# Six and five row buffers in place of three for the gathered experts of a two-layer trunk

## The chip, the cores and the metric

The kernel runs on one core of a Trainium2 chip. The core has a matrix engine (TensorE, PE in the profile; its weight loads are PEld), a vector engine (VectorE, DVE), a scalar engine (ScalarE, ACT), GpSimd (POOL) and SyncE (SP), and 16 DMA engines that move data between HBM and the on-chip buffer SBUF. Each engine works off its own list of instructions in order; semaphores make one list wait for another or for a transfer. The metric is the time on the device in microseconds, lower is better.

## The reference

Two layers (DEPTH = 2) of width 1024 run over 512 latent tokens and 256 context tokens. Each layer has token mixers and then a feed-forward part that picks 16 experts per head from 16384, with 8 heads, so 128 experts per token:

```python
q = (xc @ w_q).reshape(PEER_CHUNK, PEER_HEADS, 2, PEER_HALF)
s = jnp.einsum('thid,hikd->thik', q, sub_keys)
...                                    # top 16 of each half, then top 16 of the sums
u = u_emb[eidx]
hid = jax.nn.gelu(jnp.einsum('td,thkd->thk', xc, u))
wgt = gate * hid
return jnp.einsum('thk,thkd->td', wgt, v_emb[eidx])
```

`u_emb` and `v_emb` are tables of 16384 rows of 1024 float32 numbers. The context tokens are needed by the first layer's feed-forward part and by the second layer's keys and values; only the 512 latent tokens are returned.

## The kernel before

The kernel computes in float32 by splitting each operand into a high part (rounded on ACT, L93) and a low part (the rest, on DVE, L94), and by three matmuls for each product (L98 to L100, `mm3`). So each chunk of weights costs one ACT and one DVE instruction before PE can use its low part: `wlo` for projections, `ul` for the first expert matrix and `vl` for the second.

The feed-forward part is computed in two ways at once.

- **Dense.** For most tokens (all 512 in the first layer, 384 in the second) PE multiplies by all 16384 experts: `hidden` streams `peer_u` in 128 chunks of 512 KB (`uraw`, split to `uh`, `ul`), and `values` streams `peer_v` (`vraw`, split to `vh`, `vl`). `weigh` multiplies the hidden activations by a gate matrix, zero for the experts that were not picked, and splits the result into `wh`, `wl`.
- **Gathered.** For the 256 context tokens of the first layer and the last 128 latent tokens of the second, `gathered` fetches only the picked rows. A tile is 128 tokens. For each head it fetches 16 times one row of `peer_u` per token, and then 16 times one row of `peer_v`; one fetch is 128 rows of 4 KB, so 524 288 bytes. POOL issues the fetch as an indirect DMA (L855). DVE multiplies a `peer_u` row with the token and sums it up (L868), ACT applies the gelu, and DVE adds the weighted `peer_v` row to an accumulator (L876 for the first, L878 for the others). That is 256 fetches a tile, 512 in the first layer and 256 in the second.

In the first layer the gathered tiles lie beside the mixers of the latent tokens, their keys and top-k, `hidden` and `values`. In the second layer the gathered tile lies beside keys, gates, `hidden` and `values` of the latent tokens. In the second layer `experts` computes the first 20 chunk groups of `hidden` to memory; then it runs `hidden` for two groups at a time in turn with `values` for the two before (the loop over `c` with pool `vb`), and last `values` for the 20 stored groups (pool `vc`).

The program is written as tiles and pools; a tile pool with `bufs=3` gives three places in turn, and a new tile in a place waits until the last reader of the old one is done. A scheduler then fixes the order of each engine's list, by a model of times and by priorities. The gathered tiles have the lowest priority (`self.prio(late)` with late = 40000): their instructions go where the model finds an engine free. On the chip these lists are fixed, so a DVE instruction of the gathered tiles that waits for its row holds up all that stands behind it on DVE.

Of the kernel before, what the change touches and what calls it, by code (L numbers as in the profile page):

```python
# [21 lines left out]
F32 = mybir.dt.float32  # L22
# [10 lines left out]
P = 128  # L33
D = 1024
KT = D // P
# [34 lines left out]
class Net:  # L70
# [778 lines left out]
    def gathered(self, l, tiles, gp, gq, nat, late):  # L849

        nc, a = self.nc, self.a

        def fetch(t, idx, s):
            r = gp.tile([P, D], F32, tag="row", name="row", bufs=3)
            nc.gpsimd.indirect_dma_start(out=r, out_offset=None, in_=a[t],  # L855
                                         in_offset=bass.IndirectOffsetOnAxis(ap=idx[:, s:s + 1], axis=0))
            return r

        for row, idx, g, hsrc, i, dst in tiles:
            with self.prio(late):  # L860
                x = gp.tile([P, D], F32, name="gx", bufs=1)
                nc.sync.dma_start(x, nat[row:row + P, :])
                acc = gp.tile([P, D], F32, name="gacc", bufs=1)
                for h in range(8):
                    hid = gp.tile([P, 16], F32, name="ghid", bufs=2)
                    for k in range(16):
                        r = fetch("peer_u", idx, h * 16 + k)
                        nc.vector.scalar_tensor_tensor(out=r, in0=r, scalar=1.0, in1=x, op0=OP.mult, op1=OP.mult,  # L868
                                                       accum_out=hid[:, k:k + 1])
                    w = gp.tile([P, 16], F32, name="gw", bufs=2)  # L870
                    nc.scalar.activation(w, hid, AF.Gelu_apprx_tanh)
                    nc.vector.tensor_tensor(w, w, g[:, h * 16:h * 16 + 16], op=OP.mult)
                    for k in range(16):
                        r = fetch("peer_v", idx, h * 16 + k)
                        if h == 0 and k == 0:
                            nc.vector.tensor_scalar(acc, r, w[:, k:k + 1], None, op0=OP.mult)  # L876
                        else:
                            nc.vector.scalar_tensor_tensor(acc, r, w[:, k:k + 1], acc, op0=OP.mult, op1=OP.add)  # L878
            res = gp.tile([P, KT, P], F32, tag="row", name="gres", bufs=3)
            nc.sync.dma_start(res, hsrc.rearrange("(k p) t -> p k t", p=P))  # L880
            tr = gq.tile([P, 4, P], F32, tag="gtr", name="gtr", bufs=1)
            for k in range(KT):
                nc.tensor.transpose(tr[:, k % 4], acc[:, k * P:(k + 1) * P], self.ident)
                nc.vector.scalar_tensor_tensor(res[:, k], tr[:, k % 4], self.modT[l][:, 40 + k, i:i + 1], res[:, k], op0=OP.mult, op1=OP.add)
            nc.sync.dma_start(dst.rearrange("(k p) t -> p k t", p=P), res)
# [10 lines left out]
    def run(self):  # L896
        nc, tc, a = self.nc, self.tc, self.a
        dt = lambda name, shape=(D, NT): tc.dram_tile(list(shape), F32, name=name)
        L = range(DEPTH)
        self.pd, self.od, self.md = [[dt(f"{n}{l}") for l in L] for n in ("pd", "od", "md")]  # L900
        self.qd, self.kd = [[dt(f"{n}{l}", (NH, P, 2, NT)) for l in L] for n in ("qd", "kd")]
        self.ld = [dt(f"ld{l}", (NH, P, NT)) for l in L]
        self.vd = [dt(f"vd{l}", (2, NH, P, NT)) for l in L]
        self.hmid = [dt(f"hmid{l}") for l in L]
        self.hout = dt("hout")
        self.natd = [dt("natd0", (NC, D)), dt("natd1", (P, D))]
        self.gd = dt("gd", (NX // 32, P, P * 32))
        self.hidd = dt("hidd", (32, P, 4 * NX))
        self.EC, self.stored = 2, 20
        X, Cx = Stream(0, NX, 0), Stream(NX, NC, 1)  # L910
        with ExitStack() as root:
            self.consts(self.pool(root, "consts"))
            ges = eh = h = None
            for l in L:
                ges, eh, h = self.trunk(l, X, Cx, ges, eh, h)
                ges, eh, h = self.ffn(l, ges, eh, h)
            eh.close()
            ges.close()
# [205 lines left out]
    def experts(self, l, y, up, uq, eu, e2):  # L1124


        n, EC, S = y.n, self.EC, self.stored
        with ExitStack() as es:
            self.hidden(l, y, up, uq, range(S), 12000)
            acc = self.pool(es, f"acc{l}").tile([P, KT, n], F32, name="acc")  # L1130
            va, vq = self.pool(es, f"va{l}"), self.pool(es, f"vq{l}", 1, PSUM)
            with ExitStack() as ev:
                vb = self.pool(ev, f"vb{l}")
                for c in range(S, 32 + EC, EC):
                    if c < 32:
                        ge = self.hidden(l, y, up, uq, range(c, c + EC), 0, True)
                    if c > S:
                        cs = range(c - EC, c)
                        self.values(l, n, cs, self.weigh(l, n, va, cs, had), lambda dq: (vb, 3, vb, EC + 2), vq, acc, c == S + EC)
                    had = ge  # L1140
                eu.close()
                e2.close()
            vb = self.pool(es, f"vc{l}", side="right")
            for c in range(0, S, EC):
                cs = range(c, c + EC)
                self.values(l, n, cs, self.weigh(l, n, va, cs), lambda dq: (vb, 3, vb, EC + 2), vq, acc, False,
                            vb if c == S - EC else None)
# [73 lines left out]
```

## Time and profile before

| | before |
|---|---|
| median of 3 runs | 5116.54 us (5113.34 to 5140.52) |
| profiled execution | 5126.48 us |
| its span in the trace | 5124.7 us |
| PE busy in the span | 4846.5 us |
| DVE busy in the span | 3946.3 us |
| data moved | 1280.77 MB, 250 GB/s in the mean |

The profiled execution is 9.9 us above the median, and its span leaves 1.8 us of it outside. In a row of the wait view, the engine and instruction on the left waited for what stands right of the arrow; then come the total in us, the number of waits and the longest. In a row of windows the busy time of each engine in that stretch is given, with the number of its instructions, then the granted clock of PE (1.00 is 2.4 GHz, the lower level of 1.2 GHz counts as 0.5), the busy share of the 16 DMA engines and the data rate. In a timeline row stand the start, the duration, the instruction, and in brackets the idle time before it and what ended it.

### The profile page before, as it was taken

The numbers are of one execution on the slowest core, as the hardware profiler recorded it, in microseconds if no ns is written. First come the engines' busy times: TensorE is split into PE (matmuls) and PEld (weight loads), VectorE is DVE, ScalarE is ACT, GpSimd is POOL, SyncE is SP. The second block draws the span as 40 slices with busy tenths as digits, with TensorE's granted clock in tenths as the row PEclk, the third lists the DMA queues.
The fourth block names the chain that finished last, engine by engine and source line by source line (L and its number), as shares of the span: only waits on it lengthen the run. The fifth ranks groups of instructions, "written<-read, shape, count | busy, mean of one in ns | idle before, by whom it ended". The sixth has DMA issues, their size and how long they took to land.

```text
span 5124.7 us, 74008 instructions
## 1 busy us (share of the span) xinstructions
PE 4846.5 (95%) x27373; PEld 4187.1 (82%) x27373; DVE 3946.3 (77%) x7996; ACT 1984.5 (39%) x2970; POOL 1199.9 (23%) x1060
## 2 busy tenths in 40 slices
PE   8999999798799999989999999999999999899999
PEld 5689787576588788768888879888679889899999
DVE  5468785977799998568888766777459999787885
ACT  4346665222233344323222334555334344332333
POOL 0012000144433343243334100100000433244320
PEclk9999999899899999999999999999899999999999
DMA  8668554488888888999999734543355888988995
GB/s 308 239 201 237 179 169 129 145 271 276 281 302 270 297 300 323 323 315 320 342 335 337 261 114 161 175 135 118 120 169 173 282 297 329 319 313 292 335 330 177
DMA packets 509419, 1280.77 MB, mean 250 GB/s; under 512 B 42880, under 2 KB 225024, under 8 KB 500736
## 3 DMA queue, kind: packets, MB, share of 16 engines
q1 hardware_dynamic: 302816, 669.35, 38.7%
q0 software_dynamic: 132352, 449.90, 26.1%
q10 hardware_dynamic: 73888, 156.79, 8.2%
q8 instruction: 215, 3.52, 0.3%
q14 instruction: 148, 1.21, 0.1%
HBM read 1098.13 MB, written 177.73 MB: 249 GB/s over the span
## 4 chain that ended last, share of the span: by engine, by line
PE 47%; DMA 14%; issue 11%; DVE 9%; POOL 3%; ACT 1%; POOLq 0%; DVEq 0%; ACTq 0%; SPq 0%
DMA row<-peer_v,ix 8%; PE dps L100 6%; PE dps L99 6%; PE dps L98 6%; DMA row<-peer_u,ix 5%; PE mm L98 4%; PE mm L100 4%; PE mm L99 4%; PE hid L100 4%; PE hid L98 4%; PE hid L99 3%; POOL row L855 3%; DVE gacc L878 2%; PE gps L760 1%; PE qk L100 1%
## 5 line engine op out<-in xcount | busy, mean ns | idle before, releaser
L100 PE MATMUL hid<-yh,ul 128*128 128x512 f32 (+1 forms) x2048 | 760.8, 373 | 55.3 <-DVE ul L94 54.9
L855 POOL DMA_INDIRECT row<-peer_v,ix x384 | 586.7, 1528 | 876.9 <-DVE gacc L878 537.4
L98 PE MATMUL hid<-yh,uh 128*128 128x512 f32 (+1 forms) x2048 | 758.3, 371 | 21.0 <-ACT yh L286 13.1
L855 POOL DMA_INDIRECT row<-peer_u,ix x384 | 503.5, 1311 | 1113.7 <-DVE row L868 614.3
L99 PE MATMUL hid<-yl,uh 128*128 128x512 f32 (+1 forms) x2048 | 755.9, 369 | 3.6 <-DVE yl L287 3.6
L100 PE MATMUL dps<-wh,vl 128*128 128x512 f32 (+1 forms) x2048 | 740.9, 364 | 11.8 <-DVE vl L94 11.8
L99 PE MATMUL dps<-wl,vh 128*128 128x512 f32 (+1 forms) x2048 | 741.1, 364 | 7.0 <-DVE wl L94 7.0
L98 PE MATMUL dps<-wh,vh 128*128 128x512 f32 (+1 forms) x2048 | 735.3, 364 | 8.9 <-ACT vh L93 8.9
L98 PE MATMUL mm<-hi,whi 128*128 128x512 f32 (+1 forms) x1856 | 665.5, 359 | 19.6 <-ACT rg L481 6.0
L100 PE MATMUL mm<-hi,wlo 128*128 128x512 f32 (+1 forms) x1856 | 658.6, 357 | 25.3 <-DVE wlo L94 25.0
L99 PE MATMUL mm<-lo,whi 128*128 128x512 f32 (+1 forms) x1856 | 659.8, 356 | 1.7 <-DVE lo L94 1.7
L878 DVE SCALAR_TENSOR_TENSOR gacc<-row,gw,gacc 128x1024 f32<-128x1024 f32 x381 | 488.2, 1281 | 166.9 <-DMA row<-peer_v,ix 165.4
L868 DVE SCALAR_TENSOR_TENSOR row<-row,gx 128x1024 f32<-128x1024 f32 x384 | 466.9, 1222 | 168.5 <-DMA row<-peer_u,ix 167.9
L94 DVE TENSOR_TENSOR wlo<-wraw,whi 128x1024 fp32r<-128x1024 f32 (+1 forms) x356 | 428.1, 1204 | 178.5 <-ACT whi L93 175.7
L93 ACT ACTIVATE uh<-uraw 128x1024 fp32r<-128x1024 f32 x256 | 271.3, 1060 | 689.5 <-PE hid L99 657.4
L93 ACT ACTIVATE whi<-wraw 128x1024 fp32r<-128x1024 f32 (+1 forms) x356 | 369.9, 1043 | 385.3 <-PE mm L99 270.1
L93 ACT ACTIVATE vh<-vraw 128x1024 fp32r<-128x1024 f32 x256 | 270.1, 1057 | 633.6 <-PE dps L99 387.9
L100 PEld LDWEIGHTS hid<-yh,ul 128*128 128x128 f32 x2048 | 391.2, 191 | 107.4 <-DVE ul L94 69.3
L98 PEld LDWEIGHTS hid<-yh,uh 128*128 128x128 f32 x2048 | 392.1, 192 | 63.6 <-ACT yh L286 14.7
L100 PEld LDWEIGHTS dps<-wh,vl 128*128 128x128 f32 x2048 | 386.3, 189 | 53.2 <-DVE vl L94 12.7
L99 PEld LDWEIGHTS hid<-yl,uh 128*128 128x128 f32 x2048 | 391.4, 191 | 44.7 <-DVE yl L287 5.0
L98 PEld LDWEIGHTS dps<-wh,vh 128*128 128x128 f32 x2048 | 386.6, 189 | 49.9 <-ACT vh L93 9.7
(337 smaller groups left out, 9481.1 us busy)
## 6 DMA issues: line engine op xcount, KB each, us to landing
uraw<-uT SPq DMA_DIRECT2D x256, 512.0 KB
vraw<-v SPq DMA_DIRECT2D x256, 512.0 KB
wraw<-w_in SPq DMA_DIRECT2D x216, 512.0 KB
gd<-gst ACTq DMA_DIRECT2D x28, 2048.0 KB
mw<-w_mod SPq DMA_DIRECT2D x96, 512.0 KB
wraw<-wq SPq DMA_DIRECT2D x80, 512.0 KB
hidd<-ge ACTq DMA_DIRECT2D x128, 256.0 KB
G<-gd SPq DMA_DIRECT2D x32, 1024.0 KB
```

The costliest lines, as they stand in the source:

```text
L93: self.nc.scalar.activation(hi, src, AF.Copy)
L94: self.nc.vector.tensor_tensor(lo, src, hi.bitcast(F32), op=OP.subtract)
L98: mm(ps, lh, rh, start=start, stop=False)
L99: mm(ps, lh, rl, start=False, stop=False)
L100: mm(ps, ll, rh, start=False, stop=stop)
L760: nc.tensor.matmul(ps[:, t], A[:, a_, :, t_], B[x][:, a_, :, t_], start=x == 0, stop=x == 1)
L855: nc.gpsimd.indirect_dma_start(out=r, out_offset=None, in_=a[t], in_offset=bass.IndirectOffsetOnAxis(ap=idx[:, s:s + 1], axis=0))
L868: nc.vector.scalar_tensor_tensor(out=r, in0=r, scalar=1.0, in1=x, op0=OP.mult, op1=OP.mult, accum_out=hid[:, k:k + 1])
L878: nc.vector.scalar_tensor_tensor(acc, r, w[:, k:k + 1], acc, op0=OP.mult, op1=OP.add)
```

## The change

The row buffers (`row`, and the two short-lived `gres` tiles that use the same places) get a number of places by layer, six in the first and five in the second, where both had three. A place takes 4 KB of each SBUF partition. In the loop of `experts` over the groups that were not stored, `vh` and `vl` get three places each (EC + 1) and no longer four (EC + 2), 8 KB of a partition less in sum, as much as the second layer's two added row places take.

```diff
         def fetch(t, idx, s):
-            r = gp.tile([P, D], F32, tag="row", name="row", bufs=3)
+            r = gp.tile([P, D], F32, tag="row", name="row", bufs=self.rows[l])
...
-            res = gp.tile([P, KT, P], F32, tag="row", name="gres", bufs=3)
+            res = gp.tile([P, KT, P], F32, tag="row", name="gres", bufs=self.rows[l])
...
-        self.EC, self.stored = 2, 20
+        self.EC, self.stored, self.rows = 2, 20, (6, 5)
...
-                        self.values(l, n, cs, self.weigh(l, n, va, cs, had), lambda dq: (vb, 3, vb, EC + 2), vq, acc, c == S + EC)
+                        self.values(l, n, cs, self.weigh(l, n, va, cs, had), lambda dq: (vb, 3, vb, EC + 1), vq, acc, c == S + EC)
```

No instruction is added or removed, but the scheduler lays the lists anew. On DVE the operations of the gathered tiles (L868, L876, L878, one for each fetch) stand earlier beside the rest. Counted in DVE's list between the same marks (the n-th split of a kind), with the stretch of the trace of before that the marks enclose:

| stage | from, to (mark on DVE) | stretch, us | gather operations before | changed |
|---|---|---|---|---|
| A | first gather, 195th `wlo` | 991 to 1388 | 127 | 146 |
| B | to the 69th `ul` | 1388 to 1901 | 128 | 152 |
| C | to the 58th `vl` | 1901 to 2540 | 160 | 207 |
| D | to the end of the first layer | 2540 to 2946 | 97 | 7 |
| E | second layer, first gather, 200th `ul` | 3973 to 4279 | 71 | 85 |
| F | to the 226th `ul` | 4279 to 4435 | 32 | 43 |
| G | to the 205th `vl` | 4435 to 4797 | 109 | 119 |
| H | to the end | 4797 to 5124 | 44 | 9 |

A holds the mixers of the latent tokens, B their keys, top-k and gates beside the first part of `hidden`, C the rest of `hidden` and the start of `values`, D the rest of `values`; E is keys, gates and `hidden` of the second layer, F and G the rest of `hidden` and the loop over `c`, H the stored groups.

DVE's list in stage A, around the 188th and 189th `wlo` (splits of `w_out`; `hmid` is the projection's result, `gacc` and `row` are the gathered tile's), before:

```order
L94 TENSOR_TENSOR wlo<-wraw,whi 128x1024
L868 SCALAR_TENSOR_TENSOR row,ghid<-row,gx 128x1024 x3
L631 SCALAR_TENSOR_TENSOR hmid<-mm,modT_98,oht 128x512 x2
L94 TENSOR_TENSOR wlo<-wraw,whi 128x1024
L631 SCALAR_TENSOR_TENSOR hmid<-mm,modT_98,oht 128x512
L868 SCALAR_TENSOR_TENSOR row,ghid<-row,gx 128x1024 x2
```

and with the change:

```order
L94 TENSOR_TENSOR wlo<-wraw,whi 128x1024
L872 TENSOR_TENSOR gw<-gw,gk_11018 128x16
L878 SCALAR_TENSOR_TENSOR gacc<-row,gw,gacc 128x1024 x3
L94 TENSOR_TENSOR wlo<-wraw,whi 128x1024
L878 SCALAR_TENSOR_TENSOR gacc<-row,gw,gacc 128x1024
L631 SCALAR_TENSOR_TENSOR hmid<-mm,modT_98,oht 128x512
```

The gather is 9 operations further at the same weight split (115 of them in front of the second `wlo` here, and 106 before), and four of them, not three, stand between the first `wlo` here and the first `hmid`.

DVE's list at the border from `hidden` to `values` of the first layer, in stage C (`gel` and `wl` belong to `weigh`), before, from the 128th `ul` to the first `vl` after it:

```order
L94 TENSOR_TENSOR ul<-uraw,uh 128x1024
L809 TENSOR_TENSOR gel<-gel,G 128x512 x4
L94 TENSOR_TENSOR wl<-gel,wh 128x512
L878 SCALAR_TENSOR_TENSOR gacc<-row,gw,gacc 128x1024
L94 TENSOR_TENSOR wl<-gel,wh 128x512 x2
L868 SCALAR_TENSOR_TENSOR row,ghid<-row,gx 128x1024
L94 TENSOR_TENSOR wl<-gel,wh 128x512
L868 SCALAR_TENSOR_TENSOR row,ghid<-row,gx 128x1024 x4
L94 TENSOR_TENSOR vl<-vraw,vh 128x1024
```

and with the change:

```order
L94 TENSOR_TENSOR ul<-uraw,uh 128x1024
L878 SCALAR_TENSOR_TENSOR gacc<-row,gw,gacc 128x1024 x4
L868 SCALAR_TENSOR_TENSOR row,ghid<-row,gx 128x1024 x2
L809 TENSOR_TENSOR gel<-gel,G 128x512 x4
L94 TENSOR_TENSOR wl<-gel,wh 128x512
L868 SCALAR_TENSOR_TENSOR row,ghid<-row,gx 128x1024
L94 TENSOR_TENSOR wl<-gel,wh 128x512 x3
L868 SCALAR_TENSOR_TENSOR row,ghid<-row,gx 128x1024 x3
L94 TENSOR_TENSOR vl<-vraw,vh 128x1024
```

Ten gather operations now stand between this `ul` and this `vl`, and six did before.

## Rows read from the trace of the kernel before

**Rows 1.** Page, part 1: busy us, share of the span, instructions.

```profile
PE 4846.5 (95%) x27373; PEld 4187.1 (82%) x27373; DVE 3946.3 (77%) x7996; ACT 1984.5 (39%) x2970; POOL 1199.9 (23%) x1060
```

**Rows 2.** Waits, whole span: who waited for whom, us, times, longest.

```profile
POOL row L855 <- DVE row L868: 743.8, 273, 14.3
POOL row L855 <- DVE gacc L878: 660.8, 271, 15.0
...
DVE row L868 <- DMA row<-peer_u,ix: 167.9, 105, 7.6
DVE gacc L878 <- DMA row<-peer_v,ix: 165.4, 97, 6.4
...
PE hid L100 <- DVE ul L94: 54.9, 33, 5.8
...
PE mm L100 <- DVE wlo L94: 28.9, 16, 4.2
```

**Rows 3.** Timeline of DVE, 2283 to 2308 us.

```profile
2285.85 1.22 DVE L868 SCALAR_TENSOR_TENSOR row<-row,gx 128x1024 f32<-128x1024 f32 x1
...
2294.18 1.23 DVE L868 SCALAR_TENSOR_TENSOR row<-row,gx 128x1024 f32<-128x1024 f32 x1 [5.36 <-DMA row<-peer_u,ix]
...
2297.83 1.22 DVE L94 TENSOR_TENSOR vl<-vraw,vh 128x1024 fp32r<-128x1024 f32 x1
2303.52 1.23 DVE L868 SCALAR_TENSOR_TENSOR row<-row,gx 128x1024 f32<-128x1024 f32 x1 [4.46 <-DMA row<-peer_u,ix]
```

**Rows 4.** Timeline of POOL, 2270 to 2308 us.

```profile
2285.00 2.88 POOL L855 DMA_INDIRECT row<-peer_u,ix  x1 [3.06 <-DVE gacc L878]
...
2295.69 1.78 POOL L855 DMA_INDIRECT row<-peer_u,ix  x1 [4.81 <-DVE row L868]
```

**Rows 5.** Timeline of PE, 2292 to 2308 us.

```profile
2305.94 0.80 PE L100 MATMUL dps<-wh,vl 128*128 128x512 f32 x1 [11.04 <-DVE vl L94]
```

**Rows 6.** Windows, stages A to H: length, busy us, PE clock, DMA share, GB/s.

```profile
991.00:1388.00 397.00, 335.04 (x1348) 259.05 (x1347) 298.03 (x391) 104.26 (x131) 175.91 (x147) 0.93 0.81 273
1388.00:1901.00 513.00, 500.24 (x2936) 426.58 (x2936) 487.75 (x1337) 187.82 (x281) 190.12 (x128) 0.99 0.85 292
1901.00:2540.00 639.00, 613.48 (x3045) 501.56 (x3044) 489.42 (x650) 204.02 (x291) 221.02 (x161) 0.98 0.92 323
2540.00:2946.00 406.00, 401.23 (x1767) 329.84 (x1766) 336.37 (x449) 117.11 (x149) 133.87 (x94) 1.00 0.90 313
3973.00:4279.00 306.00, 281.30 (x1855) 267.22 (x1854) 280.72 (x638) 116.65 (x189) 120.87 (x75) 0.98 0.82 291
4279.00:4435.00 156.00, 141.94 (x1005) 136.41 (x1004) 129.42 (x178) 65.87 (x108) 49.67 (x32) 0.95 0.93 340
4435.00:4797.00 362.00, 344.86 (x1945) 341.39 (x1944) 292.31 (x398) 119.05 (x165) 147.03 (x109) 0.99 0.87 304
4797.00:5124.00 327.00, 323.67 (x1870) 323.05 (x1868) 253.43 (x373) 109.72 (x148) 57.93 (x42) 1.00 0.80 275
```

**Rows 7.** Waits of PE, stage A.

```profile
PE mm L100 <- DVE wlo L94: 28.4, 15, 4.2
```

**Rows 8.** Waits of DVE, stage A.

```profile
DVE gacc L878 <- DMA row<-peer_v,ix: 52.1, 25, 6.4
DVE row L868 <- DMA row<-peer_u,ix: 38.6, 22, 4.7
```

**Rows 9.** Page, part 5: groups of instructions, busy us, mean ns of one.

```profile
L855 POOL DMA_INDIRECT row<-peer_v,ix x384 | 586.7, 1528 | 876.9 <-DVE gacc L878 537.4
...
L878 DVE SCALAR_TENSOR_TENSOR gacc<-row,gw,gacc 128x1024 f32<-128x1024 f32 x381 | 488.2, 1281 | 166.9 <-DMA row<-peer_v,ix 165.4
L868 DVE SCALAR_TENSOR_TENSOR row<-row,gx 128x1024 f32<-128x1024 f32 x384 | 466.9, 1222 | 168.5 <-DMA row<-peer_u,ix 167.9
...
L93 ACT ACTIVATE vh<-vraw 128x1024 fp32r<-128x1024 f32 x256 | 270.1, 1057 | 633.6 <-PE dps L99 387.9
```

**Rows 10.** Windows, 20 us at the border from `hidden` to `values`.

```profile
2290.00:2310.00 20.00, 7.10 (x23) 5.04 (x22) 11.32 (x17) 4.14 (x5) 7.36 (x6) 0.62 0.98 374
```

## The prediction

> **What bounds the kernel now.** I read the page's busy times first. PE is busy for 4846.5 of 5124.7 us [rows 1], so all that can be won without fewer matmuls is PE's idle time, about 278 us, and the time that it ran at the lower clock. Where PE waits, the wait view names DVE most often: 54.9 us for `ul` and 28.9 us for `wlo`, the low parts of weights [rows 2]. DVE itself waits 167.9 + 165.4 = 333.3 us for gathered rows, and POOL waits 743.8 + 660.8 us for DVE to give a row buffer back [rows 2]. This is a ring: DVE reads a row, the buffer is free, POOL issues the next fetch, the row travels, DVE waits.
>
> One turn of it is to be seen at the border from `hidden` to `values`. POOL issues a fetch at 2295.69, after a wait for DVE [rows 4], and DVE can read that row only at 2303.52, after standing idle for 4.46 us; another wait of 5.36 us ends at 2294.18 [rows 3]. From issue to use that is 7.8 us, with 1.8 us of issue in it. Two waits of this kind stand around one `vl` split (1.22 us), and PE stands still for 11.04 us until 2305.94 for a `vl` that comes right behind the second [rows 3, 5]. Three places let three fetches pass in 2303.52 - 2294.18 = 9.3 us, one each 3.1 us. In stage A there are 127 fetches in 397 us, also 3.1 us each [rows 6]: there the ring is at its limit.
>
> **The change, part by part.** Six places give six fetches in such a turn, 9.3/6 = 1.6 us each, five give 1.9 us; POOL's own issue takes 1.53 us in the mean for `peer_v` [rows 9], so it doesn't yet bind. The lists ask for less: 146 operations in stage A, even in an unchanged 397 us, are one each 2.7 us. So I expect most of DVE's 333 us of row waits to go, at least three quarters; a burst of more than six operations in a row may still wait.
>
> What that is worth differs by stage. In each I take the length, PE's idle time (length less busy), the time lost to the clock, and three floors: PE's, DVE's with the added operations (1.3 us each, the mean of 1.22 + 0.08 and 1.28 [rows 3, 9] to one digit) and that of the DMA engines with 0.524 MB for each added fetch. For the DMA floor I divide a stage's rate by its busy share: 323/0.92 = 351 GB/s in C and 340/0.93 = 366 in F [rows 6].
>
> - **A, 397 us.** PE idles 62.0 us, and a clock of 0.93 means 14% of the stage, 56 us, at 1.2 GHz, so 28 us lost [rows 6]. DVE waits 52.1 + 38.6 = 90.7 us for rows [rows 8]; PE waits 28.4 us for `wlo` [rows 7]. The rest of PE's idle time is single waits of a norm and of others, which I leave. I take 26 us of the `wlo` waits and half of the 28: -40 us, to 357. DVE then has 298 + 19 x 1.3 = 323 us of work, and the DMA engines (273 x 397 = 108.4 MB, + 10.0) / 351 = 337 us: both fit, tightly. Bounds: -90 (all idle and clock) and 0.
> - **B, 513 us.** PE idles 12.8 and loses 5 to the clock, DVE idles 25.3; 24 added operations are 31 us on DVE. So DVE is full, and what its row waits give back is spent at once. 0, between -18 and +6.
> - **C, 639 us.** PE idles 25.5 and loses 13 to the clock (0.98), a floor of 600. DVE gets 47 x 1.3 = 61 us more, 550. But the data grow from 323 x 639 = 206.4 to 231.0 MB: 631 us at 366 GB/s, 658 at 351. I take the middle, 645: +6 us. Bounds: 618 us at the 374 GB/s of one 20 us window [rows 10], -21; and 715 at the stage's present 323 GB/s, +76.
> - **D, 406 us.** 90 operations leave it, but PE idles only 4.8 there. -3.
> - **E, 306 us.** PE idles 24.7 and loses 6 to the clock; DVE is busy for 280.7 + 14 x 1.3 = 299. So DVE allows at most -7; I take -7.
> - **F, 156 us.** PE idles 14.1 and loses 8 to the clock; the data grow from 53.0 to 58.8 MB, 161 us at 366 (+5), while DVE (129 + 14 us) has room. +3, between -22 and +17 (at the stage's 340 GB/s).
> - **G, 362 us.** PE idles 17.1 and loses 3.6; DVE has 292 + 13 = 305 us, and 115.3 MB are 328 us at 351. Nothing covers the waits but the rows: -14, between -20 and 0.
> - **H.** PE idles 3.3 of 327 us. 0.
> - **Three places for `vh` and `vl`** in the loop over `c`: the second chunk of a quarter can be split only once the first chunk of the quarter before has been read to its end. The loop has 6 x 4 quarters. If each exposes the whole split, it is 24 x (1.06 + 1.22) = 55 us [rows 3, 9]; if the matmuls of the next `hidden` chunks stand between, nothing. ACT already waits 387.9 us for PE before `vh` splits over the span [rows 9], while PE's whole idle time in F and G, where the loop lies, is 31.2 us [rows 6]; so I take a value near nothing, +4. Behind a late `vh` on ACT stand the next `uh` splits, and on DVE gather operations; PE waits for both.
>
> A page of the Trainium skill can be held against stage C. "DMA: Bandwidth & Descriptors", section "Where 436 GB/s comes from", says that for transfers between HBM and SBUF the memory's share of about 358 GB/s per core binds; its section "Measured" also has 425 GB/s for one large transfer with the other core idle. By the first, an estimate for C is 231.0/358 = 645 us and the sum stays; by the second 544 us, PE's 600 would bind, C would give 39 and the sum would be 45 us lower. The trace goes above 358 for 20 us at a time (374), and no stage of it above 340 [rows 6, 10], so the first figure is the better guide here.
>
> Sum: -40 + 0 + 6 - 3 - 7 + 3 - 14 + 0 + 4 = -51 us against the profiled 5126.5, so 5075.5. The median of the runs is 9.9 us below the profiled execution, so 5065 us.
>
> **Rivals.**
> - *DVE is the next bound, and PE gains little.* Rows no longer wait, but DVE's share of work rises to 323 of 357 us in A and to 299 of at most 306 in E, and a split behind three or four gather operations (1.3 us each) is as late as one behind a wait. For it: B, where DVE is busy for 487.8 of 513 us. Against it: in this same B, PE idles just 12.8 us. If only a third of A's and G's gains comes, it is 36 us less: -15, 5101 us. The change not doing what it says belongs here too: if an issue takes 2.88 us, as one does [rows 4], six places can't bring a fetch each 1.6 us, and the time stays at 5117.
> - *The DMA engines give no more than now.* Slower. It is one place, C: more fetches in flight take the bandwidth that `uraw`, `vraw` and the gates' loads have, these land late, and PE waits for splits whose data isn't there. At D's 313 GB/s, with a DMA share of 0.90, C's 231.0 MB need 738 us, +99 in place of +6, so +42 in sum: 5159 us. It decides below 231.0/(639 + 57) = 332 GB/s, where C eats the other 57 us. Against it: the shares of 0.90 to 0.93 are not full.
> - *All that DVE's waits hold up comes back.* Idle time and clock together are 90 us in A, 18 in B, 39 in C, 31 in E, 22 in F and 21 in G [rows 6], 221 in all; two thirds of it are 147, so 4970 us. For it: the waits in rows 3 and 5 pass on in full. Against it: the floors of DVE and DMA in A, C and E.
>
> The Trainium skill has a rule for the slow issue: "SBUF — State Buffer", section "Who interferes with whom", says that a DVE instruction with two SBUF inputs contends with a GpSimd instruction that reads SBUF, and L868 and L878 have two. The trace shows issues of 1.78 and 2.88 us here; whether DVE holds them up is not shown.
>
> **How the numbers follow.** Forecast 0.50, DVE the next bound 0.20, a slow issue 0.04, DMA 0.13, all comes back 0.13. Within 0.5% of 5116.5 (about what a measurement of this kernel can tell from no change) is 5091 to 5142. The forecast's own range is 5030 to 5090: it and the last rival are faster, 0.63; the first rival, with the slow issue, is the same, 0.24; the second is slower, 0.13. The range of 5000 to 5140 leaves out most of the DMA rival and the far part of the last, under 2 in 10. The likeliest is 5065.
>
> **What would show it.** DVE's waits for rows should fall from 333 to below 85 us, POOL's waits for DVE may stay long, since it now fetches ahead. PE's idle time in A should fall from 62 to about 36 with the clock at 0.96 or more; the 11.04 us stall at the border should be gone or below 3. The first layer's gather should end soon after the 58th `vl`. C should be no shorter than now, with a DMA share near 1 and 350 GB/s or more. If DVE's row waits stay above 200 us, or if PE's idle time in A stays above 55 while they go, the step from row waits to PE is wrong; if C grows by more than 30 us, the DMA floor was set too low; if the loop over `c` shows PE waits for `vh` or `vl` above 15 us, the third place was costed too low.

## The result, and the profile after

The changed kernel took 5055.97 us in the median of four runs (5052.75 to 5071.67); the kernel before, run beside it, took 5114.94. The ratio is 0.9879, with a 95% interval of 0.9842 to 0.9917: about 59 us faster. The profiled execution of the changed kernel is its longest run, 5071.67 us with a span of 5069.6, so it stands 54.8 us below the profiled execution of before.

Busy times, from the page; they answer to [rows 1]:

```profile
PE 4826.3 (95%) x27373; PEld 4177.0 (82%) x27373; DVE 3948.6 (78%) x7996; ACT 1989.7 (39%) x2970; POOL 1260.8 (25%) x1060
```

Waits over the whole span, in us, times and longest; they answer to [rows 2]:

```profile
POOL row L855 <- DVE row L868: 445.7, 196, 13.5
POOL row L855 <- DVE gacc L878: 445.3, 221, 14.0
...
PE dps L98 <- ACT vh L93: 34.7, 9, 26.5
...
DVE row L868 <- DMA row<-peer_u,ix: 26.8, 17, 11.0
...
PE hid L100 <- DVE ul L94: 22.3, 19, 8.2
...
DVE gacc L878 <- DMA row<-peer_v,ix: 4.9, 5, 3.2
```

DVE's waits for rows fell from 333.3 to 26.8 + 4.9 = 31.7 us. PE's waits for `ul` fell from 54.9 to 22.3, and those for `wlo` from 28.9 to next to nothing. One row is new: of 34.7 us in which PE waits for `vh`, one single wait is 26.5 us long.

The stages between the same instructions as in [rows 6], A, B, C, the first 406 us of D, E, F, G and H, in the same columns:

```profile
1000.00:1341.00 341.00, 315.53 (x1327) 252.55 (x1326) 318.67 (x425) 105.39 (x131) 207.52 (x169) 0.95 0.94 348
1341.00:1840.00 499.00, 495.89 (x2885) 423.82 (x2883) 494.33 (x1341) 182.55 (x271) 218.66 (x154) 1.00 0.90 320
1840.00:2496.00 656.00, 626.51 (x3137) 506.28 (x3137) 563.37 (x753) 212.80 (x306) 317.22 (x208) 0.98 0.98 357
2496.00:2902.00 406.00, 405.62 (x1791) 334.85 (x1791) 239.59 (x310) 119.07 (x147) 2.98 (x2) 1.00 0.61 197
3919.00:4212.00 293.00, 277.72 (x1827) 265.09 (x1826) 288.47 (x648) 113.06 (x180) 150.43 (x91) 0.98 0.90 325
4212.00:4389.00 177.00, 139.08 (x1006) 132.14 (x1004) 151.01 (x205) 68.56 (x118) 90.35 (x44) 0.89 0.94 339
4389.00:4739.00 350.00, 341.31 (x1946) 339.07 (x1945) 302.81 (x412) 119.55 (x164) 162.67 (x119) 1.00 0.93 330
4739.00:5070.00 331.00, 326.54 (x1887) 325.92 (x1885) 216.76 (x324) 110.09 (x147) 7.72 (x5) 1.00 0.64 214
```

In A, PE's idle time fell from 62.0 to 25.5 us and its clock rose from 0.93 to 0.95. B gave 13.5 us, C took 16.3, D, taken up to the first score product of the next layer, gave 11.0. E gave 14.1 and G 12.6, but F took 21.5: PE's busy time in F is no larger than before, its idle time went from 14.1 to 37.9 us. The stretch ahead of the first fetch and the trunk of the second layer were 8.9 and 1.2 us longer.

**The border in the first layer.** A timeline row of PE in the changed kernel; it answers to [rows 5]:

```profile
2241.67 2.07 PE L98 MATMUL dps<-wh,vh 128*128 128x512 f32 x4 [6.42 <-ACT wh L93]
```

And one of DVE, which answers to [rows 3]:

```profile
2240.26 2.50 DVE L809 TENSOR_TENSOR gel<-gel,G 128x512 f32<-128x512 f32 x4 [4.22 <-DMA gel<-hidd]
```

The stall of 11.04 us behind a late row is gone, but one of 6.42 us stands in its place (below 3 was forecast), and what DVE waits for in front of it is the load of `gel`. The last gather operation of the layer starts at 2514 us, 18 us behind the 58th `vl`; before it started at 2874.

**The border in the second layer.** This is F's 26.54 us. A timeline row of PE in the changed kernel:

```profile
4378.88 0.69 PE L98 MATMUL dps<-wh,vh 128*128 128x384 f32 x1 [26.54 <-ACT vh L93]
```

SP's rows ahead of it; an issue that SP holds back leaves a hole between the end of one row and the start of the next:

```profile
4334.21 20.66 SPq L777 DMA_DIRECT2D uraw<-uT  x5
4359.26 3.99 SPq L801 DMA_DIRECT2D G<-gd  x2
4363.30 8.46 SPq L826 DMA_DIRECT2D vraw<-v  x3
```

ACT's rows in the same stretch:

```profile
4349.13 0.33 ACTq L763 DMA_DIRECT2D gd<-gst  x1
4352.20 1.06 ACT L93 ACTIVATE uh<-uraw 128x1024 fp32r<-128x1024 f32 x1 [3.10 <-PE hid L99]
4370.52 1.93 ACT L93 ACTIVATE wh<-ge 128x384 fp32r<-128x384 f32 x4 [17.27 <-DVE ge L809]
4377.77 1.06 ACT L93 ACTIVATE vh<-vraw 128x1024 fp32r<-128x1024 f32 x1 [5.31 <-DMA vraw<-v]
```

And DVE's first product of `ge` and `G`:

```profile
4369.93 1.96 DVE L809 TENSOR_TENSOR ge<-ge,G 128x384 f32<-128x384 f32 x4 [3.64 <-DMA G<-gd]
```

Read from the end: PE waits for `vh`, whose `vraw` was issued on SP behind `G`. `G` stands there behind the last `uraw` of the loop's first chunks, and SP holds it until the gates' last write, issued on ACT at 4349.13, has landed. `G` itself needs 10.7 us from issue to its first use. The last split of a `uraw` is long done by then, so no `hidden` product is left to cover the way. In the kernel before, SP issued the same `G` earlier in its list; its rows there:

```profile
4365.31 37.43 SPq L777 DMA_DIRECT2D uraw<-uT  x7
4402.84 1.65 SPq L801 DMA_DIRECT2D G<-gd  x2
```

There it stood behind the layer's 97th `uraw`, now behind the 100th. From its issue to PE's first product of `values` it took 17.3 us before and 19.6 us after, but before, `hidden` products filled all but 7.07 us of it.

### The profile page after: what moved, and what is told of

Same layout as the page of the kernel before. It is cut to its first block, busy times and chain, and to the rows that moved or that the text cites. A ratio compares the mean times of both kernels' runs of the same rounds, so it can differ in the third digit from the quotient of the medians.

```text
span 5069.6 us, 73962 instructions
## 1 busy us (share of the span) xinstructions
PE 4826.3 (95%) x27373; PEld 4177.0 (82%) x27373; DVE 3948.6 (78%) x7996; ACT 1989.7 (39%) x2970; POOL 1260.8 (25%) x1060
## 3 DMA queue, kind: packets, MB, share of 16 engines
q0 software_dynamic: 132352, 449.90, 25.5%
## 4 chain that ended last, share of the span: by engine, by line
PE 71%; DVE 11%; DMA 6%; issue 6%; ACT 3%; POOL 2%; SPq 1%; ACTq 0%; DVEq 0%; POOLq 0%
PE dps L100 7%; PE dps L98 7%; PE dps L99 7%; PE mm L98 6%; PE mm L99 6%; PE hid L100 6%; PE mm L100 6%; PE hid L98 6%; PE hid L99 6%; PE qk L98 3%; PE qk L100 3%; PE qk L99 2%; DVE row L868 2%; POOL row L855 2%; PE mps L244 2%
## 5 line engine op out<-in xcount | busy, mean ns | idle before, releaser
L98 PE MATMUL dps<-wh,vh 128*128 128x512 f32 (+1 forms) x2048 | 740.6, 366 | 42.9 <-ACT vh L93 34.7
L855 POOL DMA_INDIRECT row<-peer_v,ix x384 | 616.7, 1606 | 652.1 <-DVE gacc L878 322.6
L100 PE MATMUL hid<-yh,ul 128*128 128x512 f32 (+1 forms) x2048 | 757.1, 371 | 22.5 <-DVE ul L94 22.3
L100 PE MATMUL dps<-wh,vl 128*128 128x512 f32 (+1 forms) x2048 | 735.5, 365 | 12.9 <-DVE vl L94 12.6
L855 POOL DMA_INDIRECT row<-peer_u,ix x384 | 534.9, 1393 | 746.2 <-DVE row L868 290.1
L878 DVE SCALAR_TENSOR_TENSOR gacc<-row,gw,gacc 128x1024 f32<-128x1024 f32 x381 | 486.7, 1278 | 7.4 <-DMA row<-peer_v,ix 4.9
L868 DVE SCALAR_TENSOR_TENSOR row<-row,gx 128x1024 f32<-128x1024 f32 x384 | 461.1, 1216 | 27.0 <-DMA row<-peer_u,ix 26.8
```

The lines of the kernel that those rows point to most:

```text
L98: mm(ps, lh, rh, start=start, stop=False)
L100: mm(ps, ll, rh, start=False, stop=stop)
```

## The experiments

Sums "A to D" and "E to H" are lengths between the same instructions in each profile. They were 2032.4 and 1152.1 us before, 1968.7 and 1150.3 after. Ratios are to the kernel before, run beside each, with 95% intervals; the lengths and stalls are those of one profile each. The edits are shown shortened and against the changed kernel: `rows` stands for `self.rows`, and `vb, EC + 1` for the places of `vh` and `vl`.

### Which layer, and is it the third place?

**First layer alone**

```
- rows = (6, 5);  vb, EC + 1
+ rows = (6, 3);  vb, EC + 2
```

> Six row places in the first layer, three in the second, and the four places for vh and vl as before. Up to the second layer's experts its order of instructions is that of the changed kernel. Theory (each layer has its own account, and the first holds nearly all of the gain): stage A near 341 us, B 499, C 656, D 473, as in the changed kernel, and E to H together as in the kernel before, 1152 us; so 5055 to 5062 us, 0 to +6 against the changed kernel. Rival 1 (the second layer's five places give what E and G show, 27 us, and F's loss belongs to the third place for vh and vl alone): E to H 1152, no stall of over 10 us at the border from hidden to values, total as in the theory. Rival 2 (F's loss comes from the order at the border: the load of G stands behind the 80th uraw and the last gd write; here it stands so too): a PE stall of over 12 us at that border again, with four places for vh and vl, and F above 165 us.

5083.1 us, ratio 0.9914 (0.9885 to 0.9943). A to D 1971.9, as in the changed kernel; E to H 1166.0, 14 us more than before. The border shows a stall of 24.51 us, with four places for `vh` and `vl`; `G` stands behind the 100th `uraw` here too. So rival 2 held: the stall isn't the third place's. The theory's total of 5055 to 5062 us was missed: it took E to H at 1152 us.

**Second layer alone**

```
- rows = (6, 5)
+ rows = (3, 5)
```

> Three row places in the first layer, five in the second, three places for vh and vl. The first layer runs in the order of the kernel before. Theory: stages A to D as before (397, 513, 639, 484 us), the second layer as in the changed kernel, E 292, F 170 to 180, G 350: within 5 us of the kernel before, 5110 to 5118. Rival (the layers act on each other, the second layer's gain needs the first's): E, F or G differ by more than 10 us from the changed kernel's. Of F: the G load stands behind the 80th uraw here as well, and the gates end later against hidden (the last evacuation of a gate behind 94 splits, not 91), so if the border's order makes the stall it is 20 us or more here too.

5112.68 us, ratio 0.9976 (0.9960 to 0.9992). A to D 2021.9. E 285.5, F 177.1, G 347.4, H 331.3: E and G gain, and a stall of 31.82 us at the border takes most of it.

**Third place alone**

```
- rows = (6, 5)
+ rows = (3, 3)
```

> Three row places in both layers, three places for vh and vl in the loop over c: only the place is taken away, and the order of instructions is that of the kernel before up to that loop. If the place costs what the prediction took, F and G are 4 us longer together and the total is 5119. If the place makes F's +21 us, F is above 172 us and the total above 5130, with PE waits for vh above 25 us. If the border's order makes it, F stays at 150 to 160 us, PE waits for vh below 12 us, total 5113 to 5122. At most, each of the 24 quarters exposes a split: +55 us, 5170.

5122.48 us, ratio 1.0001 (0.9986 to 1.0015). F 156.0. PE's row at the border:

```profile
4430.00 0.69 PE L98 MATMUL dps<-wh,vh 128*128 128x384 f32 x1 [7.07 <-ACT vh L93]
```

That is the 7.07 us of the kernel before: the place costs nothing that can be measured (F and G together are 1.3 us shorter; the interval of the total is 7 us wide to either side). Both this run and the one before it have the order of the kernel before up to the second layer, and 998 to 1000 us ahead of the first fetch; so the 8.9 us there (991.4 to 1000.3) are a spread between runs and not the change's.

### How many places?

**Five**

```
- rows = (6, 5);  vb, EC + 1
+ rows = (5, 3);  vb, EC + 2
```

> Five row places in the first layer, three in the second, four for vh and vl. Theory (a ring: a turn of 9.3 us and k places give a fetch each 9.3/k us, 1.9 us for five; stage A now asks for one each 341/146 = 2.3 us): five suffice in the mean; DVE's row waits in A below 25 us, A 340 to 355 us, total 5055 to 5072. Rival (the six places matter for bursts: up to six gather operations stand in a row on DVE): DVE row waits in A 35 us or more, A about 360 to 370 us, total 5075 to 5090.

5052.74 us, ratio 0.9863 (0.9829 to 0.9897). A 352.1, with 23.1 us of row waits, as the theory had it; the total is 2 us below its range. In this run `G` stands behind the 97th `uraw`, the stall at the second border is 7.07 us, and E to H are 1146.1: with three places in the second layer it is as fast as the changed kernel. The three totals with three places there (this run, the first layer alone, and four places below) differ more by the border's order (E to H 1146.1, 1166.0, 1159.9) than by the first layer's places (A to D 1962.3, 1971.9, 1968.3).

**Four**

```
- rows = (6, 5);  vb, EC + 1
+ rows = (4, 3);  vb, EC + 2
```

> Four row places in the first layer, three in the second, four for vh and vl. By the ring a turn of 9.3 us and four places give a fetch each 2.3 us, just what stage A asks for (341 us/146). Theory: some half of three places' row waits in A stay, 30 to 50 us, A 360 to 375 us, A to D 1985 to 2010, total 5080 to 5100. Rival (the fourth place is all it needs, the turn is shorter when POOL need not wait): A 345 to 355, total within 10 us of five places. At the second layer's border G stands behind the 100th uraw, so a stall of 20 us or more is expected there, as in the other orders with it.

5077.1 us, ratio 0.9912 (0.9895 to 0.9928). A 365.8, with 43.6 us of row waits, as the theory had it, but A to D is 1968.3, below what it allowed. Its windows of A, B and C:

```profile
993.00:1359.00 366.00, 322.26 (x1329) 254.04 (x1328) 312.02 (x413) 105.35 (x131) 189.03 (x161) 0.95 0.89 314
1359.00:1860.00 501.00, 496.51 (x2932) 424.09 (x2932) 489.81 (x1347) 186.06 (x278) 204.85 (x135) 1.00 0.86 305
1860.00:2479.00 619.00, 605.12 (x3045) 496.68 (x3044) 503.27 (x660) 205.59 (x294) 252.16 (x174) 0.99 0.95 344
```

| places, first layer | DVE's row waits, A to D | PE idle, A to D, less the last wait (6.2 us) | A | C | A to D |
|---|---|---|---|---|---|
| 3 (before) | 231.6 us | 105.2 us | 396.6 | 639.5 | 2032.4 |
| 4 | 62.5 | 62.2 | 365.8 | 618.6 | 1968.3 |
| 5 | 39.4 | 55.5 | 352.1 | 647.0 | 1962.3 |
| 6 (after) | 12.8 | 58.6 | 341.1 | 655.8 | 1968.7 |

The fourth place brings the whole gain: in the other profiles A to D are 1964.0 with four, 1964.4 and 1966.5 with five, and 1968.9 to 1972.7 with six. The next two take another 50 us of waits from DVE, and what A (24.7 us) and D (9.5) gain by them, C gives back (37.2). In A itself PE's idle time goes with DVE's row waits: 62.0 us beside 90.8 with three places, 43.7 beside 43.6 with four, 30.9 beside 23.1 with five and 25.5 beside 11.7 with six. Each depth comes with lists of its own, though, and no run has more places with the lists of before, so the first layer's gain is not split between shorter waits and another order. The 5077.1 us of this run come from its second layer: E to H are 1159.9, with a stall of 21.06 us at the border, where `G` again stands behind the 100th `uraw`.

### Do the DMA engines bind C?

```
+ if l == 0 and c >= 17:
+     nc.sync.dma_start(raw[:, :4].rearrange("p k e -> p (k e)"), a["uT"][l, 4 * c + e][:, :4 * P])
+     v4 = lambda z: z.rearrange("p (a k) e -> p a (k e)", a=2)
+     self.split(v4(uh), v4(ul), v4(raw)[:, 0:1].to_broadcast([P, 2, 4 * P]))
+ else:
      ...                                  # load and split as before
```

> The changed kernel, where the chunks from 17 on of the first layer's hidden load only half of each block of uT (0.26 MB in place of 0.52; the half is used twice, so the result is left wrong there): some 59 loads, 15 MB of stage C's 234 MB are gone; the matmuls, splits and gathers are all there, and the order is the same up to the start of C. Theory (the DMA engines bind C): 15 MB at 357 GB/s are 43 us, and PE's idle time and clock there, 29.5 + 13.7 us, are what it can give: C falls by 25 to 43 us, ACT's waits for vraw from 59 to below 20 us. Rival (C is bound by splits that stand behind gather operations on DVE, or by the order): C falls by less than 10 us.

One run: 5064.1 us. Its window of C:

```profile
1834.00:2476.00 642.00, 615.78 (x3100) 498.96 (x3101) 571.06 (x757) 207.65 (x302) 320.21 (x208) 0.98 0.95 343
```

C is 13.7 us shorter, between what the theory and the rival allowed, but 38 products of `values` moved out of it into D, some 8 us at the 0.23 us from one to the next, and D is 7.3 us longer. PE's idle time is 26.2 us against 29.5. ACT's waits for `vraw` are 50.2 us, where the theory wanted them below 20.

The bytes were taken from `hidden`, so only ahead of the border. C in two parts, up to the first product of `values` and from there, in the changed kernel:

```profile
1840.00:2221.00 381.00, 371.08 (x2066) 301.42 (x2065) 319.06 (x419) 138.58 (x210) 196.53 (x120) 0.99 0.97 360
2221.00:2496.00 275.00, 255.43 (x1071) 204.87 (x1072) 244.31 (x335) 74.22 (x97) 120.69 (x89) 0.96 0.99 354
```

and in this run:

```profile
1834.00:2218.00 384.00, 370.70 (x2064) 301.63 (x2065) 334.67 (x447) 134.62 (x209) 216.47 (x134) 0.99 0.93 335
2218.00:2476.00 258.00, 245.08 (x1037) 197.34 (x1038) 236.39 (x311) 73.03 (x94) 103.74 (x75) 0.97 0.99 354
```

Where the bytes were taken, C is 3 us longer, although its data fell by some 9 MB (13 more gather operations came ahead of the border). So there the bytes don't set the length, at a DMA share of 0.97; but PE had only 9.9 us of idle time to give there. All that C lost came behind the border, where no load was cut, 38 products and 8 gather operations fewer are left, and the share stays 0.99 at 354 GB/s. Whether the DMA engines bind that part this run doesn't test. In the changed kernel ACT waits there for `vraw`, and before it waited for PE; this is before, over stage C:

```profile
ACT vh L93 <- PE dps L99: 114.9, 27, 8.9
ACT vh L93 <- DMA vraw<-v: 14.8, 4, 8.8
```

and after:

```profile
ACT vh L93 <- DMA vraw<-v: 59.3, 15, 9.9
ACT vh L93 <- PE dps L99: 12.6, 2, 7.9
```

### The stall at the border

**The changed kernel again**

> The changed kernel again, on the chip and in the call of the three runs that follow. If nothing differs by chip: 5053 to 5062 us, a ratio near 0.988, F with its one stall of 20 us or more before the first matmul of values.

5064.17 us (5055.82 to 5076.68), ratio 0.9870 (0.9851 to 0.9888). F 180.0, stall 28.71. The median is 2 us above what was expected, the ratio as expected.

**Gates earlier, 13000**

```
  for t in range(nd - 1, -1, -1):
+     with self.prio(-13000 * l):
          i1, i2, g = self.pick(ep, tv[t], ti[t])
          self.slots_t(...)
          for b in range(4):
              self.gates(...)
```

> The changed kernel with one edit: in the second layer pick, slots_t and gates get an earlier priority (13000), so that in the order the last evacuation of a gate stands behind 88 splits of uh where it stood behind 91, and G is loaded two uraw earlier. Nothing else is moved before that layer's experts. Theory (the stall of 26.5 us comes from G waiting behind the gates' last write): F falls from 177 to 150 to 160 us, PE's waits for vh from 34.7 to below 15, total 15 to 25 us below the changed kernel of this call. Rival (the stall is the price of a DVE that is full of gather operations, or of six gather operations in a row at the border): F stays above 168 us and the total within 8 us.

5058.81 us (5045.11 to 5065.85), ratio 0.9861 (0.9837 to 0.9886). F 159.5, stall 15.49, but E is 301.5, 8 us longer than in the run above. In the medians it is 5 us faster than the run above, less than the theory wanted, and the ranges overlap: F went by the theory, the total by the rival.

**Five places in both layers, gates earlier**

```
- rows = (6, 5)
+ rows = (5, 5)   # and prio(-13000 * l), as above
```

> Five row places in both layers, three for vh and vl, and the gates' earlier priority as in the run before. Theory: A to D as with five places (352, 490, 647, 473), E to H with the second layer's five places without the stall (290, 152, 350, 330): 10 to 30 us below the changed kernel, 5025 to 5045. Rival: the border keeps its stall (the gates end behind 90 splits here, not 88), F above 168, total 5045 to 5060.

5067.62 us, ratio 0.9886 (0.9868 to 0.9903): outside both ranges. F is 163.6. `G` stands behind the 99th `uraw` and the stall is 23.50 us. (The splits counted in these expectations are rows of the program's order, where repeats are one row; by the trace the last gate's write stands behind 93 splits before, 96 after, 93 and 94 in the two runs with 13000, and 91 in those with 39000.)

**Gates earliest, 39000**

```
- prio(-13000 * l)   # the run with 13000
+ prio(-39000 * l)
```

> The changed kernel with the gates' priority at 39000 in the second layer: the first load of G stands behind the 96th uraw of that layer (97 before, 100 in the changed kernel, 98 and 99 in the two runs with 13000). Theory: the PE stall at the border goes with that place, 7.07 us at 97, 15.5 at 98, 23.5 at 99, 24 to 32 at 100; so 7 us or less here, F 145 to 155 us, and E to H 10 to 20 us below the changed kernel: 5040 to 5055. Rival (earlier gates take DVE's time from the splits in E): E grows by 10 us or more (292.5 to 302 or above), and the total stays within 5 us of the run with 13000.

5041.06 us (5039.24 to 5043.35), ratio 0.9840 (0.9823 to 0.9856). SP's timeline rows at the border in this run:

```profile
4340.05 0.33 SPq L777 DMA_DIRECT2D uraw<-uT  x1
4340.49 3.86 SPq L801 DMA_DIRECT2D G<-gd  x2
4344.69 8.80 SPq L826 DMA_DIRECT2D vraw<-v  x3
4353.53 0.91 SPq L806 DMA_DIRECT2D gel<-hidd  x2
4354.54 4.21 SPq L777 DMA_DIRECT2D uraw<-uT  x3
```

And PE's first product of `values` there:

```profile
4360.76 0.69 PE L98 MATMUL dps<-wh,vh 128*128 128x384 f32 x1 [8.25 <-ACT vh L93]
```

Three `uraw` now stand behind `G`. The way from its issue to the first product is still 20.3 us, but 8.25 of it are left as a stall. E, F and G in the columns of the stages:

```profile
3920.00:4225.00 305.00, 280.95 (x1858) 266.18 (x1857) 299.23 (x667) 116.09 (x188) 161.64 (x93) 0.98 0.88 322
4225.00:4376.00 151.00, 137.53 (x985) 131.78 (x984) 137.31 (x183) 66.32 (x108) 70.35 (x41) 0.97 0.99 369
4376.00:4711.00 335.00, 333.92 (x1922) 333.60 (x1921) 295.70 (x405) 119.19 (x164) 155.41 (x113) 1.00 0.94 337
```

E is 12 us longer than after, as the rival said, but F is 26 and G 15 shorter: E to H are 1121.1 us, 29 below the changed kernel, and the total is 18 us below the run with 13000, where the rival wanted it within 5.

**Five and four places, gates earliest**

```
- rows = (6, 5)
+ rows = (5, 4)   # and prio(-39000 * l)
```

> Five row places in the first layer, four in the second, three for vh and vl, the gates' priority at 39000: G stands behind the 96th uraw, the last gd write behind some 87 splits. Theory: A to D as with five places (1962 to 1966 us), the border's stall 7 us or less, E to H 1125 to 1140: 5030 to 5050, the lowest of all. Rival: four places let DVE wait for rows again in the second layer, 25 us or more, and E to H is 1145 or above, total above 5050.

5044.42 us, ratio 0.9856 (0.9838 to 0.9873). A to D 1964.4, E to H 1133.3, stall 7.41: within the theory, but no lower than the run above, and DVE waits 37 us for rows in the second layer, as the rival had it.

**Four and five places, gates earliest**

```
- rows = (6, 5)
+ rows = (4, 5)   # and prio(-39000 * l)
```

> Four row places in the first layer, five in the second, three for vh and vl, the gates' priority at 39000; G stands behind the 96th uraw. Theory (from the fourth place on the first layer's length no longer depends on the places: A to D were 2032 us with three, 1968 with four, 1961 to 1966 with five, 1969 to 1973 with six): A to D 1960 to 1975 us although DVE waits for rows some 60 us there (13 with six), E to H near 1121 as with six and five, the total within 8 us of it: 5033 to 5049. Rival (the equal sum at four was luck of one order of instructions): A to D 1985 or more, total 5058 or above.

5042.06 us, ratio 0.9834 (0.9808 to 0.9859). A to D 1964.0, with 68 us of row waits on DVE; E to H 1130.5, 9 more than expected. It equals the version with six, two row buffers (8 KB of each partition) cheaper. The three runs with 39000 (5041 to 5044 us, their ranges overlap) are the fastest of the study, below both kernels. No run has three places in the second layer with 39000, so what its fourth and fifth place add to that order is open.

Over all runs the stall goes with the place of `G` on SP: 5.25, 7.41 and 8.25 us behind the 96th `uraw`, 7.07 (three times) behind the 97th, 15.49 behind the 98th, 23.50 behind the 99th, and 21.06 to 31.97 (six times) behind the 100th. What goes with the place is how many products of `hidden` PE still has between the issue of `G` and the first product of `values`: 66 to 68, 45 to 50, 21, none and none, from the 96th to the 100th. From the 97th to the 96th nothing more is gained: the way itself was 15.9 to 17.3 us in the three runs with the 97th, all with three places in the second layer, and 18.9 to 20.3 us in those with the 96th.

## Why the prediction was right, and where it was not

The time was right, 5065 against 5056, and so was the ring that it rested on. DVE's row waits fell to 31.7 us (below 85 was asked), and the gain lies in the first layer, where most of them went. But that the sum came out so close is in part luck: A to D gave 63.6 us where 37 stood, E to H 1.7 where 14 stood, and 10.1 us were lost outside the stages. Several terms were wrong, in part against each other.

- **A, -40, was -55.5.** PE's idle time fell by 36.5 us, where 26 was expected; the clock came to 0.95, not 0.96. PE's busy time there fell by 19.5 us too, in part by the clock and in part because 18 products (1345 to 1327) now stand outside the two marks, which is no gain. DVE was busy for 318.67 us, as forecast (323).
- **B, 0, was -13.5, C, +6, was +16.3.** Both are largely one move: 96 products of the gates went from B into C, and 24 of `values` from D into C. C's busy time rose by 13.0 us, its idle time by 4.0. B to D together are 8.2 us shorter, where +3 stood. B's own term failed in one point: DVE is full there (494.33 of 499), as was said, yet PE's idle time fell from 12.8 to 3.1 us. Here a full DVE delayed PE less than one that also waited 21 us for rows.
- **C's mechanism was not shown.** The step "the data are 231 MB, 645 us" put the DMA engines as the bound of the whole stage. The data came so (357 GB/s for 656 us, 234 MB) with a share of 0.98. But ahead of the border fewer bytes gave nothing, and PE idles little there; part of the added length is the work moved in. Behind the border the step may hold; no run decides it. The two sizes of the Trainium skill that were weighed there ("DMA: Bandwidth & Descriptors", "Where 436 GB/s comes from") therefore don't decide the part ahead of the border; the rate of 357 agrees with its figure of about 358, but 369 GB/s over 151 us, in the run with the gates earliest, does not fit it as a ceiling.
- **D, -3, was -11.0,** of which the 24 products moved to C are 5 us.
- **E, -7, was -14.1, G, -14, was -12.6.** DVE allowed more in E than was thought; its idle time there is 4.5 us.
- **F, +3, was +21.5.** The step failed that reckoned F by data and DVE alone. The new order puts `G` three `uraw` later on SP, behind the gates' last write, and nothing covers its way. This is a change of order, and it could have been read ahead: SP's order of the two kernels differs at that place.
- **Three places, +4, were 0.** By the prediction's own sign (PE waits for `vh` above 15 us in the loop) the place would have been blamed. The run of the place alone shows 7.07 us, unchanged, and the run of the first layer alone, with four places for `vh` and `vl`, shows the stall again.
- **H, 0, was +3.4**; ahead of A and in the second layer's trunk 10.1 us more, the larger part of it spread.

Of the rivals, "DVE is the next bound" has its sign right in B and E, where DVE is idle for 4.7 and 4.5 us, but not its price. The slow issue did not bind: POOL still waited 891 us for DVE. The DMA rival needed C below 332 GB/s, and C ran at 357. The rival by which all comes back wanted 147 us, and 59 came. What stays open is why the fifth and sixth place give C back what A and D gain. The counts show that C then holds more gather operations (173, 191, 208) and more PE idle time (13.9, 22.5, 29.5), and that its part behind the border grows (245, 256, 275 us), but no run takes these operations, or their bytes, out of that part alone.

## What to carry to other kernels

When a ring of buffers starves an engine, count its turn and the demand: here a turn of 9.3 us over four places is one fetch each 2.3 us, what stage A asks for. Four places gave the whole gain, and those beyond moved idle time from one stage to the next. A change of depth also makes the scheduler write another order, so a new stall is to be tried against the order (what stands ahead of the late load on its queue) before it is put down to the buffer that was given up; here that order was worth 29 us of E to H (1150.3 to 1121.1), and the second layer's rows 16 at the same place of `G` (1166.0 to 1150.3). A busy share of 0.97 does not say that the DMA engines are the bound: take bytes away and see, in the part where the engine that matters stands idle, and look at the parts of the stage one by one.

## What the runs showed of the hardware

The 16 DMA engines held 357 GB/s for 656 us and 369 GB/s for 151 us on this one core, where before they gave 374 for 20 us [rows 10] and 340 at most over a stage [rows 6]. Inside stage C of the changed kernel it was 374 for 150 us:

```profile
1990.00:2140.00 150.00, 142.42 (x793) 114.89 (x791) 116.29 (x144) 55.76 (x81) 71.87 (x47) 0.98 1.00 374
```

POOL's issue of a `peer_v` fetch took 1528 ns in the mean before [rows 9] and 1606 with the change:

```profile
L855 POOL DMA_INDIRECT row<-peer_v,ix x384 | 616.7, 1606 | 652.1 <-DVE gacc L878 322.6
```

It does not simply follow the number of places: the run of the first layer alone, with six there, has 1487.

A load of `G` at the second border (0.79 MB) took 9.9 to 13.4 us from issue to first use in these runs, where a row of 0.52 MB was in use 7.8 us after its issue [rows 3, 4].
